# Differential-attention step on one core: queries are projected first, engines write the stacked keys and half of each stacked query tile, and key, query and bias tiles exist twice

## The chip, the core and the metric

The kernel runs on one core of one Trainium2 chip. The metric is the time of one execution on the device in microseconds (us); for the kernel before it is the median of three runs. The profile is one further view of one execution, taken by the hardware profiler.

The core's engines are named as in the profile: PE (TensorE matmul), PEld (its weight load), DVE (VectorE), ACT (ScalarE), POOL (GpSimd) and SP (SyncE, which here issues all DMAs of the program in one order). L212 is line 212 of the kernel.

## The reference

One layer of a hybrid encoder, for 16 meta tokens, 2048 new frames (the prompt) and 32 frames of a running stream (the sample, with 528 cached rows). All arrays are float32.

```python
def diff_attend(q, k, v, q_pos, k_pos, lam, rel_bias):
    s = jnp.einsum('bqhcd,bkhcd->bchqk', q, k, preferred_element_type=f32) * SCALE
    bias = rel_bias[rel_bucket(k_pos[None, :] - q_pos[:, None])]
    s = s + jnp.transpose(bias, (2, 0, 1)).astype(f32)[None, None]
    vis = chunk_id(k_pos)[None, :] <= chunk_id(q_pos)[:, None]
    s = jnp.where(vis, s, NEG)
    p = jax.nn.softmax(s, axis=-1)
    a = p[:, 0] - lam * p[:, 1]
    return jnp.einsum('bhqk,bkhd->bqhd', a.astype(v.dtype), v)

# one layer
q, k, v, z_a, b_g, c_g, u, z_c = split_proj(rmsnorm(hp, norm_g[l]), w_in[l])   # 1024 -> 8 x 512
o = diff_attend(q, k, v, ...)                 # 4 heads, 2 components of 64 per head, values of 128
u_pad = jnp.concatenate([zeros, c_g * u], axis=1)
o = rmsnorm(o, subln_g[l]) * (1 - lam_init) * silu(z_a)
y_c = silu(z_c) * b_g * short_conv(u_pad, conv_w[l])
hp = hp + jnp.concatenate([o, y_c], axis=-1) @ w_out[l]
y_prompt = rmsnorm(hp, final_g)
```

Keys, values and the last convolution rows are outputs too.

## The kernel before

**Precision.** A float32 product is made of three products of a shorter format (float32r): each operand is split into a high part (a cast, written by ACT) and a low part (operand minus high part, by DVE or POOL), and high·high, high·low and low·high are summed in PSUM.

**Stages.** The prompt is worked in four passes `p` of 512 frames (`QT`); pass 0 also holds the 16 meta tokens and the 32 sample frames (560 columns, in two blocks). In a pass, `unit_a(h, p)` projects keys, values, queries and the gate Z of head `h` (in this order), `attend(h, p, st)` does the attention of that head over all frames so far, and `unit_c(u, p)` does the convolution branch of 128 channels with four more projections. A projection (`proj`) of one 128-column weight tile is 24 matmuls per block (8 pieces of the 1024 inputs times three products). After the passes, `out_first` and `out_rest` do the output projection.

**Keys and queries.** A score needs q·k over 64 dimensions of one component `c`. To use all 128 rows of the array, one tile `ks{c}` holds the 64 rows of the keys' high part and, below them, the 64 rows of their low part; `q{c}0` holds the queries' high part twice and `q{c}1` their low part twice. Two matmuls (L428, L429) then give the scores of up to 512 keys. The projections write 128 rows with both components (tiles of the pool `rp`, named `r` in the profile: `kh`, `kl`, `qh`, `ql`), and DMAs move the halves to where they belong:

```python
for c in range(2):
    for i, src in enumerate((kh, kl)):
        if p > 0:
            dma(ks[c][64 * i:64 * i + 64, :k0], ksd[h][i, 64 * c:64 * c + 64, :k0])      # L243
        dma(ks[c][64 * i:64 * i + 64, k0:k0 + kn], src[64 * c:64 * c + 64, :kn])         # L244
...
for half in range(2):
    dma(q2[64 * half:64 * half + 64], src[64 * c:64 * c + 64, f0:f0 + QT])               # L325
```

So a head issues four DMAs `ks<-r`, from pass 1 on four DMAs `ks<-ksd` (keys of the passes before, kept in DRAM as `ksd`), up to pass 2 two DMAs `ksd<-r`, eight DMAs `q<-r`, and one `bz<-bz` (the negated bias of the last 512 columns, L731). `ks0`, `ks1`, the four `q` tiles and `bz` exist once: a DMA that writes them waits until the scores of the head before have read them.

**Scores.** For each tile of 128 queries, `softmax_diff` makes the scores piece by piece into one of three PSUM banks `s`; DVE adds the bias and takes the minimum (L375, last piece) or the minimum alone (L378), ACT writes the exponential (L379), POOL (L382) and DVE (L383) combine both components. A bank is free when ACT has read it.

**Weights.** `w_load` brings a weight tile (`wr`, tag `wraw`, two buffers, 512 KB) and splits it: `wh` by ACT (L191), `wl` by POOL or DVE (L192).

**Order.** A scheduler orders the instructions of each engine at build time by a simulated timeline; code order sets the dependences and the rotation of buffers. Each engine runs its own order strictly, and so does SP's queue: a DMA that waits holds back all DMAs behind it. DMAs use eight semaphores in rotation (`DMAHW0` to `DMAHW7`), so a DMA may also wait for the one eight places ahead.

## Time and profile before

| what | value |
|---|---|
| three runs | 1340.38, 1341.1 and 1345.33 us, median 1341.1 us |
| profiled execution | span 1338.5 us (first to last instruction); its own time is not listed apart from that |
| PE busy | 1285.5 us (96%), 7058 matmul records |
| DVE, ACT, POOL busy | 999.3 (75%), 717.6 (54%), 682.8 us (51%) |
| granted TensorE clock, mean | 0.990 |
| DMA | 215.59 MB, 54.7% of 16 engines' time |

The median of the runs is 2.6 us above the span. In the profile a group row reads: line, engine, operation, output<-inputs, shape, count | busy us, mean ns of one | idle time of the engine before them. A row of waits reads: who waited <- whom for: us in total, times, longest. In a timeline, a bracket at the end of a row is the idle time before it and what ended it.

### The profile page before, as it was taken

To read this page: it belongs to the slowest core of one execution; us is meant where nothing else is said; L and a number is where in the kernel's file an instruction comes from. 1 tells how busy PE (TensorE), PEld (TensorE's weight loads), DVE (VectorE), ACT (ScalarE), POOL (GpSimd) and SP (SyncE) were. 2 spreads that over 40 slices of the span, in tenths; PEclk is the share of its full clock that TensorE was granted. 3 is DMA by queue.
4 is the path that set the end of the run, shared out by engine and by line. 5 is a ranking of instruction groups with operands and counts; after the bars stand their busy time and mean duration, and the time that the engine had idled before them with its cause. 6 is when DMAs were issued, how large, how long until landed. Compare 5 with 4: busy or idle time off the path is not lost.

```text
span 1338.5 us, 21190 instructions
## 1 busy us (share of the span) xinstructions
PE 1285.5 (96%) x7058; PEld 1104.2 (82%) x7058; DVE 999.3 (75%) x2086; ACT 717.6 (54%) x1814; POOL 682.8 (51%) x619
## 2 busy tenths in 40 slices
PE   8899999999999999999999999998999999999997
PEld 6899999977878878878878788887887877878875
DVE  8677676668887958788888898786785895777753
ACT  5554454555564547454645566465554665674432
POOL 4555556455555663565566535564574573452200
PEclk9999999999999999999999999999999999999999
DMA  8754543894445377545453463636247348445851
GB/s 276 229 155 125 164 117 104 245 274 138 139 147 158 103 209 232 141 151 150 150 135 126 120 208 93 167 124 143 94 110 203 117 160 215 165 150 185 273 196 52
DMA packets 118670, 215.59 MB, mean 161 GB/s; under 512 B 19840, under 2 KB 48032, under 8 KB 118560
## 3 DMA queue, kind: packets, MB, share of 16 engines
q1 hardware_dynamic: 118560, 214.23, 54.7%
q8 instruction: 56, 0.92, 0.3%
q14 instruction: 54, 0.44, 0.1%
HBM read 145.62 MB, written 43.26 MB: 141 GB/s over the span
## 4 chain that ended last, share of the span: by engine, by line
PE 59%; DVE 16%; DMA 10%; issue 4%; ACT 4%; POOL 3%; SPq 2%; DVEq 0%; POOLq 0%; ACTq 0%
PE pj L212 37%; PE po L676 6%; DVE p L383 3%; PE s L428 3%; DMA q<-r 3%; PE s L429 3%; PE pt L444 3%; SPq L73 2%; DVE nm L378 2%; PE po L452 2%; PE po L453 2%; PE po L451 2%; DMA ks<-ksd 1%; ACT p L379 1%; POOL wl L192 1%
## 5 line engine op out<-in xcount | busy, mean ns | idle before, releaser
L212 PE MATMUL pj<-xh,wh 128*128 128x512 f32 (+2 forms) x1280 | 457.0, 358 | 4.0 <-ACT wh L191 1.3
L192 POOL TENSOR_TENSOR wl<-wr,wh 128x512 fp32r<-128x512 f32 x240 | 328.7, 1375 | 250.2 <-ACT wh L191 234.7
L212 PE MATMUL pj<-xl,wh 128*128 128x512 f32 (+2 forms) x1280 | 455.1, 356 | 0.8 <-DVE xl L140 0.8
L212 PE MATMUL pj<-xh,wl 128*128 128x512 f32 (+2 forms) x1280 | 454.7, 356 | 0.0
L379 ACT ACTIVATE p<-s,nm 128x384 f32<-128x384 f32 (+5 forms) x352 | 208.8, 595 | 186.8 <-DVE nm L378 135.1
L212 PEld LDWEIGHTS pj<-xh,wh 128*128 128x128 f32 x1280 | 243.2, 190 | 34.2 <-ACT bvec L586 2.0
L212 PEld LDWEIGHTS pj<-xh,wl 128*128 128x128 f32 x1280 | 242.9, 190 | 31.2 <-issue 1.3
L212 PEld LDWEIGHTS pj<-xl,wh 128*128 128x128 f32 x1280 | 243.4, 190 | 30.1 <-DVE xl L140 1.4
L191 ACT CAST wh<-wr 128x512 fp32r<-128x512 f32 x256 | 157.0, 616 | 129.4 <-PE pj L212 78.6
L383 DVE SCALAR_TENSOR_TENSOR p<-p,cf,p 128x384 f32<-128x384 f32 (+5 forms) x176 | 174.5, 1019 | 28.1 <-POOL p L382 27.8
L428 PE MATMUL s<-ks,q 128*128 128x384 f32 (+5 forms) x352 | 129.5, 375 | 26.8 <-DMA q<-r 10.0
L382 POOL TENSOR_SCALAR p<-p,cf 128x384 f32<-128x384 f32 (+5 forms) x176 | 125.0, 726 | 49.2 <-DVE cf L359 35.1
L378 DVE TENSOR_REDUCE nm<-s 128x1 f32<-128x400 f32 (+3 forms) x224 | 122.5, 557 | 28.2 <-PE s L429 27.9
L429 PE MATMUL s<-ks,q 128*128 128x384 f32 (+5 forms) x352 | 124.0, 354 | 2.0 <-DMA q<-r 2.0
L448 DVE TENSOR_TENSOR al<-pt,ah 128x512 fp32r<-128x512 f32 x144 | 97.0, 682 | 37.0 <-ACT ah L447 36.9
L656 POOL TENSOR_TENSOR cll<-ct,chh 128x512 fp32r<-128x512 f32 x40 | 53.9, 1353 | 113.6 <-ACT chh L654 105.4
L428 PEld LDWEIGHTS s<-ks,q 128*128 128x128 f32 x352 | 66.2, 190 | 42.5 <-issue 14.4
L447 ACT CAST ah<-pt 128x512 fp32r<-128x512 f32 x144 | 79.1, 585 | 40.8 <-PE pt L444 40.7
L375 DVE CUSTOM_DVE_ANT_0 s<-s,bz 128x512 f32<-128x512 f32 (+5 forms) x128 | 74.4, 585 | 17.9 <-PE s L429 13.5
L444 PE MATMUL pt<-ident,p 128*128 128x128 f32 x544 | 86.5, 274 | 0.0
L452 PE MATMUL po<-al,vh 128*128 128x256 f32 x288 | 84.2, 292 | 1.9 <-DVE al L448 1.7
L451 PE MATMUL po<-ah,vh 128*128 128x256 f32 x288 | 81.6, 283 | 0.0
(243 smaller groups left out, 2138.4 us busy)
## 6 DMA issues: line engine op xcount, KB each, us to landing
wr<-in_w_in SPq DMA_DIRECT2D x128, 512.0 KB, 4.1
q<-r SPq DMA_DIRECT2D x128, 128.0 KB, 4.7
ct<-cat SPq DMA_DIRECT2D x28, 512.0 KB, 4.8
out<-y SPq DMA_DIRECT2D x32, 256.0 KB, 3.4
ks<-ksd SPq DMA_DIRECT2D x16, 388.0 KB, 7.8
xr<-in_x SPq DMA_DIRECT2D x24, 256.0 KB, 4.8
out<-g SPq DMA_DIRECT2D x24, 256.0 KB, 4.5
xt<-in_xT SPq DMA_DIRECT2D x24, 256.0 KB, 4.2
```

The costliest lines, as they stand in the source:

```text
L191: S.copy(wh, wi)
L192: (V if (col in (CK, CV) if p == 0 else col in (CQ, CZ)) else G).tensor_tensor(wl, wi, f32(wh), op=ALU.subtract)
L212: T.matmul(ps, lhsT=a[:, k % 4], rhs=b[k][:, b0:b1], start=(k == 0 and i == 0), stop=(k == KT - 1 and i == 2))
L378: V.tensor_reduce(nm[:, c, j:j + 1], s, op=ALU.min, axis=AX.X)
L379: S.activation(pr[j][c], s, AF.Exp, bias=nm[:, c, j:j + 1], scale=-1.0, accum_out=l[:, c, j:j + 1])
L382: G.tensor_scalar(a0, a0, cf[:, 0, j:j + 1], 1.0, op0=ALU.mult, op1=ALU.mult)
L383: V.scalar_tensor_tensor(a0, a1, cf[:, 1, j:j + 1], a0, op0=ALU.mult, op1=ALU.add)
L428: T.matmul(ps, lhsT=qd[c][0][:, qs], rhs=ks[c][:, col:col + w], start=True, stop=False)
L429: T.matmul(ps, lhsT=qd[c][1][:, qs], rhs=ks[c][:, col:col + w], start=False, stop=True)
L444: T.transpose(pt[:, i, P * qi:P * (qi + 1)], cols(aa[qi], NM + P * (2 * j + i), P), ident)
L451: T.matmul(po, lhsT=vh[:, kt], rhs=ah[:, i], start=(kt == 0), stop=False)
L452: T.matmul(po, lhsT=vh[:, kt], rhs=al[:, i], start=False, stop=False)
```

## The change

`unit_a` now projects queries first, then keys, values and Z. After a projection, ACT writes the high part of each component directly to its place, in two casts of 64 rows, and POOL the low part in two subtractions of 64 rows. For the keys both parts reach their rows this way: component 0 has its high part in rows 0 to 63 and the low part in rows 64 to 127, component 1 the other way round, so that ACT stays in its rows and POOL writes the other half. For the queries the engines write half of each of the four tiles, and four DMAs of 64 rows copy it to the other half. `ks0`, `ks1`, the `q` tiles and `bz` have two buffers, `wraw` three; the pool `rp` is gone. The past keys come in two DMAs of 128 rows, issued ahead of the key projection; `bz` is loaded ahead of `unit_a`. In pass 0 the low part of the query weights is made by DVE and that of the value weights by POOL (before: value weights by DVE, query weights by POOL). The squares at the start use the key buffers, `post` uses the buffers of `ah` and `al`, and the weights of the second output half use the key and query buffers.

```diff
-    rp = pool("rp", 5)
+    ks_tile = lambda c: kv.tile([P, NK], F32R, tag=f"ks{c}", name=f"ks{c}", bufs=2)
...
-        wr = wp.tile([P, KT, P], F32, tag="wraw", name="wr")
+        wr = wp.tile([P, KT, P], F32, tag="wraw", name="wr", bufs=3)
...
-            (V if (col in (CK, CV) if p == 0 else col in (CQ, CZ)) else G).tensor_tensor(wl, wi, f32(wh), op=ALU.subtract)
+            (V if (col in (CQ, CK) if p == 0 else col in (CQ, CZ)) else G).tensor_tensor(wl, wi, f32(wh), op=ALU.subtract)
...
+        q32 = g_tile(tw)
+        qd = [[one.tile([P, QT], F32R, tag=f"q{c}{i}", name=f"q{c}{i}", bufs=2) for i in range(2)] for c in range(2)]
+        def ev_q(ps, b0, b1):
+            V.scalar_tensor_tensor(q32[:, b0:b1], ps, -0.125, rbs[p][:, b0:b1], op0=ALU.mult, op1=ALU.mult)
+            e = min(b1, f0 + QT)
+            for c in range(2):
+                r = slice(64 * c, 64 * c + 64)
+                hi, lo = (t_[r, b0 - f0:e - f0] for t_ in qd[c])
+                S.copy(hi, q32[r, b0:e])
+                G.tensor_tensor(lo, q32[r, b0:e], f32(hi), op=ALU.subtract)
...
+        proj(CQ + h, p, ev_q)
+        for c in range(2):
+            r, o = slice(64 * c, 64 * c + 64), slice(64 - 64 * c, 128 - 64 * c)
+            for t_ in qd[c]:
+                dma(t_[o], t_[r])
+        k32 = g_tile(tw)
+        ks = [ks_tile(c) for c in range(2)]
+        if p > 0:
+            for c in range(2):
+                dma(ks[c][:, :k0], ksd[h][c, :, :k0])
         def ev_k(ps, b0, b1):
             V.tensor_tensor(k32[:, b0:b1], ps, rbs[p][:, b0:b1], op=ALU.mult)
-            S.copy(kh[:, b0:b1], k32[:, b0:b1])
-            G.tensor_tensor(kl[:, b0:b1], k32[:, b0:b1], f32(kh[:, b0:b1]), op=ALU.subtract)
+            e = min(b1, kn)
+            for c in range(2):
+                r, o = slice(64 * c, 64 * c + 64), slice(64 - 64 * c, 128 - 64 * c)
+                d = slice(k0 + b0, k0 + e)
+                S.copy(ks[c][r, d], k32[r, b0:e])
+                G.tensor_tensor(ks[c][o, d], k32[r, b0:e], f32(ks[c][r, d]), op=ALU.subtract)
         proj(CK + h, p, ev_k)
-        for c in range(2):
-            for i, src in enumerate((kh, kl)):
-                if p > 0:
-                    dma(ks[c][64 * i:64 * i + 64, :k0], ksd[h][i, 64 * c:64 * c + 64, :k0])
-                dma(ks[c][64 * i:64 * i + 64, k0:k0 + kn], src[64 * c:64 * c + 64, :kn])
         if p < NQ - 1:
-            for i, src in enumerate((kh, kl)):
-                dma(ksd[h][i, :, k0:k0 + kn], src[:, :kn])
+            for c in range(2):
+                dma(ksd[h][c, :, k0:k0 + kn], ks[c][:, k0:k0 + kn])
...
-    for col in (CK, CV)[:1]:
-        pre[col, 0] = w_load(col, 0)
+    pre[CQ, 0] = w_load(CQ, 0)
...
+            bz = one.tile([P, 512], F32, tag="bz", name="bz", bufs=2)
+            if (h, p) != (0, 0):
+                dma(bz, bzd[h])
             st = unit_a(h, p)
...
-            st["bz"] = one.tile([P, 512], F32, tag="bz", name="bz", bufs=1)
-            dma(st["bz"], bzd[h])
```

The program issues 630 DMAs instead of 782: 64 instead of 128 copies into `q` tiles, and 24 instead of 112 DMAs into `ks` tiles. How the order moves is shown at three places. In the rows, a number behind a name tells buffers apart.

SP's queue in pass 3 at head 1, before: the query tile `q00_11094` and the key tiles `ks0_10992`, `ks1_10993` wait for PE, that is, for the scores of head 0.

```order
L73 DMA q00_11094<-r_11053 64x512 [waits DMAHW0_49,PE_49]
L73 DMA ks0_10992<-ksd1_132 64x1552 [waits PE_49]
L73 DMA ks0_10992<-r_10951 64x512
L73 DMA ks0_10992<-ksd1_132 64x1552 [waits DMAHW3_49]
L73 DMA ks0_10992<-r_10952 64x512
L73 DMA q00_11094<-r_11053 64x512 [waits DMAHW5_49]
L73 DMA q01_11097<-r_11054 64x512 [waits DMAHW6_49]
L73 DMA q01_11097<-r_11054 64x512 [waits DMAHW7_49]
L73 DMA wr_12025<-in_w_in 128x1024 [waits DMAHW0_49,Pool_49]
L73 DMA ks1_10993<-ksd1_132 64x1552 [waits DMAHW1_49,PE_49]
```

The same head in SP's queue now (`ks0_10889`, `ks1_10890`, `bz_10837` and the tiles `q00_10840` to `q11_10843`).

```order
L72 DMA ks0_10889<-ksd1_129 128x1552 [waits DMAHW5_49,PE_49]
L72 DMA out_4<-g_10671 128x2 [waits DMAHW6_49,DVE_49]
L72 DMA wr_10935<-in_w_in 128x1024 [waits DMAHW7_49,DMAHW2_49,Pool_49]
L72 DMA ks1_10890<-ksd1_129 128x1552 [waits PE_49]
L72 DMA bz_10837<-bz1_301 128x512 [waits DMAHW1_49,DVE_49]
L72 DMA wr_10987<-in_w_in 128x1024 [waits DMAHW3_49,Pool_49]
L72 DMA wr_11581<-in_w_in 128x1024 [waits DMAHW4_49,Pool_49]
L72 DMA cat3_139<-g_10753 512x1x128 [waits DVE_49]
L72 DMA q00_10840<-q00_10840 64x512 [waits DMAHW5_49,Activation_49]
L72 DMA q10_10842<-q10_10842 64x512 [waits DMAHW6_49,Activation_49]
L72 DMA wr_11618<-in_w_in 128x1024 [waits DMAHW7_49,Pool_49]
L72 DMA q01_10841<-q01_10841 64x512 [waits DMAHW0_49,Pool_49]
```

The block of DMAs that followed the last reader of the only buffer is gone: past keys and bias stand well ahead of the query copies, and the query copies wait for the engines that write the first half, no longer for PE.

POOL's order at the same head, before: L236 makes the keys' low part, L314 the queries', L277 the values'.

```order
L192 TENSOR_TENSOR wl_11063<-wr_11056,wh_11062 128x512 [waits PE_49,Activation_49]
L236 TENSOR_TENSOR r_10952<-g_10950,r_10951 128x512 [waits DMAHW3_49,Activation_49]
L192 TENSOR_TENSOR wl_11111<-wr_11108,wh_11110 128x512 [waits DMAHW1_49,PE_49,Activation_49]
L192 TENSOR_TENSOR wl_11115<-wr_11108,wh_11114 128x512 [waits PE_49,Activation_49]
L277 TENSOR_TENSOR vl_10123<-v32_10131,vh_10122 128x512 [waits DMAHW6_49,DVE_49,PE_49]
```

And now (L252 the queries, L278 the keys, L313 the values).

```order
L197 TENSOR_TENSOR wl_10942<-wr_10935,wh_10941 128x512 [waits PE_49,Activation_49]
L252 TENSOR_TENSOR q01_10841<-g_10839,q00_10840 64x512 [waits DMAHW1_49,Activation_49]
L252 TENSOR_TENSOR q11_10843<-g_10839,q10_10842 64x512 [waits Activation_49,Pool_49]
L197 TENSOR_TENSOR wl_10990<-wr_10987,wh_10989 128x512 [waits PE_49,DMAHW2_49,Activation_49,Pool_49]
L197 TENSOR_TENSOR wl_10994<-wr_10987,wh_10993 128x512 [waits PE_49,Activation_49]
L278 TENSOR_TENSOR ks0_10889<-g_10888,ks0_10889 64x512 [waits Activation_49,Pool_49]
L278 TENSOR_TENSOR ks1_10890<-g_10888,ks1_10890 64x512 [waits Activation_49]
L313 TENSOR_TENSOR vl_10065<-v32_10073,vh_10064 128x512 [waits DVE_49,DMAHW5_49,PE_49,Pool_49]
```

Two subtractions stand where one stood, and those of the keys stand behind two weight subtractions (L197) that wait for ACT and PE.

SP's queue at the start, before: `wr_421` is the weight tile of the values, the second that PE needs.

```order
L73 DMA bd0_294<-bvec_171 128x383 [waits DMAHW7_49,Activation_49]
L73 DMA bd1_302<-bvec_175 128x383 [waits DMAHW0_49,Activation_49]
L73 DMA kts_415<-in_ckT 128x512 [waits DMAHW1_49]
L73 DMA bd2_310<-bvec_179 128x383 [waits DMAHW2_49,Activation_49]
L73 DMA ktn_417<-in_ckT 128x16 [waits DMAHW3_49]
L73 DMA wr_421<-in_w_in 128x1024 [waits DMAHW4_49]
```

And now: `wr_416` belongs to the keys, `wr_496` to the values, which PE still takes second.

```order
L72 DMA bd0_287<-bvec_168 128x383 [waits DMAHW7_49,Activation_49]
L72 DMA bd1_295<-bvec_172 128x383 [waits DMAHW0_49,Activation_49]
L72 DMA wr_416<-in_w_in 128x1024 [waits DMAHW1_49]
L72 DMA bd2_303<-bvec_176 128x383 [waits DMAHW2_49,Activation_49]
L72 DMA kts_490<-in_ckT 128x512 [waits DMAHW3_49]
L72 DMA ktn_492<-in_ckT 128x16 [waits DMAHW4_49]
L72 DMA wr_496<-in_w_in 128x1024 [waits DMAHW5_49]
```

The value weights have one more weight tile in front of them.

More of the change, by code (lines that the diff above doesn't have):

```diff
@@ L124, in x_rms, with sqt @@
         rbs[p] = rb
-    sqt = lambda n: rp.tile([P, 560], F32, tag="r", name="sq")[:, :n]
+    def sqt(k, n):
+        if k == 0:
+            sqs[:] = [f32(t_)[:, 560 * j:560 * (j + 1)] for t_ in [ks_tile(c) for _ in range(2) for c in range(2)] for j in range(3)]
+        return sqs[k][:, :n]
+    sqs = []
     def x_load(p):
@@ L236, in ev_k @@
-            G.tensor_tensor(kl[:, b0:b1], k32[:, b0:b1], f32(kh[:, b0:b1]), op=ALU.subtract)
+            e = min(b1, kn)
[4 more added lines that the diff above has]
+                G.tensor_tensor(ks[c][o, d], k32[r, b0:e], f32(ks[c][r, d]), op=ALU.subtract)
         proj(CK + h, p, ev_k)
         dma(kT_p[h, :, k0:k0 + kn], k32[:, :kn])
-        ks = [kv.tile([P, NK], F32R, tag=f"ks{c}", name=f"ks{c}") for c in range(2)]
@@ L240, in unit_a @@
[L240 to L244 removed]
         if p < NQ - 1:
[L246 to L247 removed]
+            for c in range(2):
+                dma(ksd[h][c, :, k0:k0 + kn], ks[c][:, k0:k0 + kn])
@@ L303, in unit_a @@
         st["v"] = (vh, vl)
-        qh, ql, q32 = r_tile(tw), r_tile(tw), g_tile(tw)
-        qs = None
-        if p == 0:
-            qs = one.tile([P, 2 * NS], F32, tag="qs", name="qs")
-            G.memset(qs, 0.0)
-        def ev_q(ps, b0, b1):
-            V.scalar_tensor_tensor(q32[:, b0:b1], ps, -0.125, rbs[p][:, b0:b1], op0=ALU.mult, op1=ALU.mult)
-            S.copy(qh[:, b0:b1], q32[:, b0:b1])
-            G.tensor_tensor(ql[:, b0:b1], q32[:, b0:b1], f32(qh[:, b0:b1]), op=ALU.subtract)
-            if p == 0 and b1 == tw:
-                for c in range(2):
-                    V.tensor_copy(qs[64 * c:64 * c + 64, NS * c:NS * (c + 1)], q32[64 * c:64 * c + 64, smp])
-        proj(CQ + h, p, ev_q)
-        qd = []
-        for c in range(2):
-            pair = []
-            for i, src in enumerate((qh, ql)):
-                q2 = one.tile([P, QT], F32R, tag=f"q{c}{i}", name=f"q{c}{i}")
-                for half in range(2):
-                    dma(q2[64 * half:64 * half + 64], src[64 * c:64 * c + 64, f0:f0 + QT])
-                pair.append(q2)
-            qd.append(pair)
-        st["q"] = qd
-        st["qs"] = qs
         z32, l1 = g_tile(tw), g_tile(tw)
@@ L631, in w_half @@
         else:
-            ks = [kv.tile([P, NK], F32R, tag=f"ks{c}", name=f"wo{c}") for c in range(2)]
+            ks = [ks_tile(c) for c in range(2)]
             his = [ks[k // 4][:, 512 * (k % 4):512 * (k % 4 + 1)] for k in range(KT)]
-            los = [r_tile(512) for _ in range(4)]
-            los += [one.tile([P, QT], F32R, tag=f"q{c}{i}", name=f"wq{c}{i}") for c in range(2) for i in range(2)]
+            los = [one.tile([P, QT], F32R, tag=f"q{c}{i}", name=f"wq{c}{i}", bufs=2) for _ in range(2) for c in range(2)
+                   for i in range(2)]
         for k in range(KT):
@@ L643, in load_cat @@
     def load_cat(t, rows, spare=False):
-        ct = wp.tile([P, KT, P], F32, tag="wraw", name="ct")
+        ct = wp.tile([P, KT, P], F32, tag="wraw", name="ct", bufs=3)
         dma(ct[:, :, :rows], cat_s if t == 16 else cat[t // 4][:, t % 4])
```

21 lines of the change are left out of this document (15 added, 6 removed).

## The prediction, made before the changed kernel was run

> **What bounds the kernel now.** I read the page's head first: busy times of the engines, the granted clock in 40 slices, and the chain of work that ended last, by engine.
>
> ```profile
> PE 1285.5 (96%) x7058; PEld 1104.2 (82%) x7058; DVE 999.3 (75%) x2086; ACT 717.6 (54%) x1814; POOL 682.8 (51%) x619
> PEclk9999999999999999999999999999999999999999
> PE 59%; DVE 16%; DMA 10%; issue 4%; ACT 4%; POOL 3%; SPq 2%; DVEq 0%; POOLq 0%; ACTq 0%
> ```
>
> PE is the bound, and the change takes no matmul away. So a gain can come from PE's idle 53.0 us (1338.5 - 1285.5) and from what idling does to the matmuls behind it, and from nothing else. Second view: PE's waits, longest in total first (total us, times, longest).
>
> ```profile
> PE s L428 <- DMA q<-r: 10.0, 6, 3.2
> PE s L428 <- ACT p L379: 8.6, 11, 2.1
> PE s L428 <- DMA bz<-bz: 4.9, 1, 4.9
> PE pv L584 <- DMA oh<-in_ohd: 4.0, 1, 4.0
> PE s L428 <- DMA ks<-r: 2.5, 1, 2.5
> PE s L429 <- DMA q<-r: 2.0, 5, 0.6
> ```
>
> Scores (`s`) that wait for DMAs of `q`, `ks` and `bz` are 10.0 + 4.9 + 2.5 + 2.0 = 19.4 us in 13 waits, the largest group; `oh` is the start of the program and stays. Third view: the timeline of SP's queue and of PE at one of these places, head 1 of pass 3.
>
> ```profile
> 1012.74 0.50 SPq L73 DMA_DIRECT2D q<-r  x1
> 1013.29 0.59 SPq L73 DMA_DIRECT2D ks<-ksd  x1
> ...
> 1020.24 0.59 SPq L73 DMA_DIRECT2D ks<-ksd  x1
> 1022.15 0.46 SPq L73 DMA_DIRECT2D ks<-r  x1
> 1022.75 1.15 SPq L73 DMA_DIRECT2D q<-r  x2
> ...
> 1020.22 0.39 PE L212 MATMUL pj<-xl,wh 128*128 128x512 f32 x1
> 1023.34 0.42 PE L428 MATMUL s<-ks,q 128*128 128x400 f32 x1 [2.73 <-DMA q<-r]
> ...
> 1026.32 0.63 PE L212 MATMUL pj<-xh,wl 128*128 128x512 f32 x1
> ...
> 1028.11 0.40 PE L212 MATMUL pj<-xh,wl 128*128 128x512 f32 x1
> ```
>
> The reader is to see two things. The DMAs into the single buffers begin only when the head before is done with them and take more than 10 us in SP's one queue; PE has filler work for 7.9 us of that and then stands. And after the stall a matmul of 512 columns lasts 0.63 instead of 0.40 us: the clock. Fourth view: the granted clock in the stretches behind three of these stalls, and in a quiet one (us, busy time of the engines, PEclk, DMA share, GB/s).
>
> ```profile
> 501.00:505.00 4.00, 3.91 (x11) 3.12 (x12) 2.00 (x4) 2.43 (x5) 0.00 (x0) 0.57 1.03 304
> 1023.80:1027.20 3.40, 3.40 (x10) 2.62 (x9) 0.00 (x0) 0.59 (x1) 0.00 (x0) 0.50 1.01 210
> 1122.90:1126.00 3.10, 3.10 (x9) 2.40 (x8) 3.10 (x5) 1.21 (x3) 1.45 (x1) 0.50 1.03 217
> 508.00:512.00 4.00, 4.00 (x20) 3.35 (x19) 2.72 (x7) 2.87 (x10) 0.00 (x0) 1.00 0.62 200
> ```
>
> **The change, part by part.**
>
> *A. Waits for q, ks and bz: -21.6 us.* With two buffers, past keys and bias are asked for a head earlier, and new keys need no DMA at all. The query copies no longer wait for PE, and are four instead of eight. What is late next at these places is the engine chain behind a projection (C). The idle time is 19.4 us. A wait also hides the tail of the matmul ahead of it, since matmuls overlap:
>
> ```profile
> L212 PE MATMUL pj<-xh,wh 128*128 128x512 f32 x768 | 305.6, 399 | 0.0
> 1130.72 4.16 PE po L676 x18
> ```
>
> One lasts 0.399 us, but 18 in a row take 4.16, 0.231 each; 13 waits hide 13 x (0.399 - 0.231) = 2.2 us more. Bounds: 0 (all waits are replaced) and 21.6. I take all of it here and count the replacement in C.
>
> *B. Half clock behind the stalls: -5.0 us.* In the three stretches the lost time is stretch x (1 - clock): 4.00 x 0.43 + 3.40 x 0.50 + 3.10 x 0.50 = 5.0 us. Bounds 0 (another stall at the same places) and 5.0; I take 5.0, because the clock is 1.00 wherever PE runs on. [...]
>
> *C. Double casts and subtractions: +5.1 us.* The number of splits doubles; the rows of before are these.
>
> ```profile
> L235 ACT CAST r<-g 128x512 fp32r<-128x512 f32 (+1 forms) x20 | 10.9, 543 | 8.7 <-DVE g L234 8.7
> L313 ACT CAST r<-g 128x512 fp32r<-128x512 f32 (+1 forms) x20 | 10.7, 536 | 3.5 <-DVE g L312 2.9 <-DMA ks<-ksd 0.6
> L236 POOL TENSOR_TENSOR r<-g,r 128x512 fp32r<-128x512 f32 (+1 forms) x20 | 23.8, 1190 | 64.9 <-ACT r L235 43.1 <-DMA ks<-r 16.5 <-DMA xr<-in_x 5.3
> L314 POOL TENSOR_TENSOR r<-g,r 128x512 fp32r<-128x512 f32 (+1 forms) x20 | 23.4, 1168 | 4.6 <-ACT r L313 3.9 <-POOL wl L192 0.7
> q<-r SPq DMA_DIRECT2D x128, 128.0 KB, 4.7
> ```
>
> No row shows these with 64 rows; I take the time to go with the columns, as the full price (half of it is the other bound, if it went with the rows). ACT then gets 20 x 0.543 + 20 x 0.536 = 21.6 us more (739, 55% of the span), POOL 20 x 1.190 + 20 x 1.168 = 47.2 us more (730, 55%). Neither binds by its sum. On the path they show only as a longer chain: for keys DVE's evacuation (taken as long as a cast, 0.54) + two casts 1.1 + two subtractions 2.4 = 4.0 us, for queries 4.7 more for the DMA, 8.7 us. The cover is the projections that stand between: queries have keys and values behind them (48 matmuls of 0.231, 11 us), keys have the values' 24 (5.5 us), and longer where scores of the head before are mixed in. In the order, the thinnest cover is the first head of pass 1 with the values' 24 matmuls, a few of the keys' and some ten small products between its queries and its first score, some 8 us; there the copies may come 1 us late. New keys are also needed last, in the last piece of a row of scores. If the cover were gone, each of the 16 heads would pay up to 4 us.
> What stays is that ACT and DVE, which until now caught up while PE stood, are now the next to be late. The price of such a wait is the row of ACT above, 8.6 / 11 = 0.78 us. I let half of the 13 places have one: 13 x 0.5 x 0.78 = 5.1 us. Bounds: 0, and the longest such wait at all 13, 13 x 2.1 = 27.3.
>
> *D. Start: +1 us.* PE's second projection, the values, now has one more weight tile ahead of its own in SP's queue and in ACT's, and its low part comes from POOL.
>
> ```profile
> 20.83 1.14 ACT L191 CAST wh<-wr 128x512 fp32r<-128x512 f32 x2 [3.62 <-DMA wr<-in_w_in]
> 25.15 2.53 POOL L192 TENSOR_TENSOR wl<-wr,wh 128x512 fp32r<-128x512 f32 x2 [8.64 <-ACT wh L191]
> 22.68 2.05 PE L158 MATMUL pss<-sq,ones 128*128 128x280 f32 x8
> ```
>
> The casts begin when the weights land, 20.83; with 1.14 us of casts for the keys' tile ahead, POOL's first subtraction would end near 20.83 + 1.14 + 0.57 + 1.27 = 23.8, the second near 25.1. PE comes to the values at 24.4, behind the squares' sums, and reaches the second half of the weights some 1.5 us later. So 0 to 2 us are lost, and I take 1.
>
> *E. At nothing.* The third `wraw` buffer: a PE wait for `wh` is not among the longest, shown above, and ACT's waits for weights lie beside PE's matmuls. The fewer bytes in the DMA queue: hidden as long as PE does not wait for a DMA. `post` in the buffers of `ah`: its matmuls and copies lie between two heads, where PE has projections. The second half of the output weights, which can load earlier: in PE's rows above there is no wait for it.
>
> The sum is -21.6 - 5.0 + 5.1 + 1.0 = -20.5 us on a span of 1338.5. The median of the runs is 1341.1, 2.6 us above the span; on it the sum gives 1320.6, which I round to 1321.
>
> **Rivals.**
>
> *R1, the wait changes its name (no change).* [...] These copies of DVE differ in little but their place in time:
>
> ```profile
> L317 DVE COPY qs<-g 64x32 f32<-64x32 f32 x8 | 6.6, 821 | 0.2
> L515 DVE COPY g<-hist 128x2 f32<-128x2 f32 x16 | 3.6, 226 | 0.0
> ```
>
> A copy of 32 columns that takes 0.821 us stood beside something, and L317 follows in the code right on POOL's subtraction of the queries' low part (L314). The price: 13 places with a wait midway between 0.78 and 2.1, 1.44 us, 18.7 us in all, and the clock halved behind them as now: -21.6 + 18.7 = -2.9, 1338 us. Against it: even if DVE stood through all 47.2 us, it would be busy 1046.5 us, 78% of the span. [...]
>
> *R2, POOL's queue holds back the keys (slower).*
>
> ```profile
> POOL wl L192 <- ACT wh L191: 234.7, 112, 8.6
> L192 POOL TENSOR_TENSOR wl<-wr,wh 128x512 fp32r<-128x512 f32 x240 | 328.7, 1375 | 250.2 <-ACT wh L191 234.7 <-ACT nm L354 6.3 <-PE pj L212 4.4
> ```
>
> For: in POOL's strict order the keys' two subtractions stand behind two weight subtractions, which wait for ACT 234.7 / 112 = 2.1 us a time. Two of them uncovered in front of the keys, 2 x 1.375 = 2.75 us at all 16 heads, is 44 us: -26.6 + 44 = +17.4, 1358 us. It decides from 26.6 / 16 = 1.7 us per head. Against: the pair already stood ahead of the keys before, and POOL is idle 45% of the time.
>
> *R3, nothing comes back (faster still).* C at 0 and D at 0, and half of ACT's 8.6 us go too, because scores start at an even pace: -26.6 - 4.3 = -30.9, 1310 us. For: 11 waits on ACT come partly behind the stalls. Against: ACT has more to do.
>
> **How the numbers follow.** My forecast (1313 to 1331) has 0.62, R1 0.16, R2 0.08, R3 0.14. The range of 8 in 10 reaches from 1306, a little below R3, to 1338, R1; outside lie R2 and the ends of R1 and R3. 0.5% of 1341.1 is 6.7 us, about what a measurement tells from no change: faster is below 1334.4. Forecast, R3 and the better end of R1 give 0.79 faster; the rest of R1 and the start of R2 0.14 the same; R2 0.07 slower.
>
> **What would show it.** A: no PE wait for `q`, `ks` or `bz` above 1 us, PE busy about 97.5% of the span. B: PEclk 1.00 around the heads' first scores. C: 40 casts and 40 subtractions each for queries and keys, about 0.54 and 1.18 us each; PE's waits for ACT and DVE together grow by about 5 us. D: PE's idle time in the first 40 us within 2 us of now. Wrong: PE waits for POOL's `ks` rows (R2), or idle time of PE as large as before under new names (R1).

## The result, and the profile after

The changed kernel takes 1328.78 us (median of 4 runs, 1327.2 to 1330.27); beside it on the same chip the kernel before took 1343.21 us (1340.38 to 1346.31). The ratio is 0.9889, with a 95% interval of 0.9864 to 0.9914: faster by 1.1%. The profiled execution has a span of 1327.7 us, 10.8 less than before. The kernel before has 57 more runs, beside the experiments below: their spans lie 1.7 to 1.9 us under their times, and their median is 1344.9 us. The profile before, with a span of 1338.5, thus belongs to a run of some 1340.3 us, and the two profiles show only 10.8 of the 14.4 us between the medians.

First the head of the page: busy times, granted clock, and the chain of work that ended last.

```profile
PE 1281.4 (97%) x7058; PEld 1105.9 (83%) x7058; DVE 1000.8 (75%) x2086; ACT 740.3 (56%) x1854; POOL 732.1 (55%) x659
...
PEclk9999999999999999899999999999999999999999
...
PE 69%; DVE 17%; ACT 5%; DMA 4%; issue 3%; POOL 1%; SPq 1%; DVEq 0%; ACTq 0%; POOLq 0%
```

PE is still the bound. DMA fell from 10% to 4% of the chain; DVE stayed, and is now what PE meets next. The same shows in PE's waits (us in total, times, longest).

```profile
PE po L686 <- DVE y L687: 5.4, 4, 2.1
PE s L438 <- ACT p L389: 5.3, 8, 3.3
PE pv L594 <- DMA oh<-in_ohd: 4.6, 1, 4.6
PE pt L454 <- DVE p L393: 4.3, 4, 2.5
PE ptv L308 <- DVE g L297: 3.9, 4, 2.2
...
PE s L439 <- DMA q<-q: 2.0, 1, 2.0
```

Of the 13 waits of scores for DMAs one is left, `q<-q`. Adding up all rows of this view by who is waited for:

| PE waits for | before, us (times) | after, us (times) |
|---|---|---|
| DMA at the start (`oh`) | 4.0 (1) | 4.6 (1) |
| other DMAs | 19.4 (13) | 2.0 (1) |
| ACT | 11.5 (14) | 5.9 (9) |
| DVE | 8.6 (16) | 25.6 (24) |
| POOL and issue | 0.6 (2) | 0 |

The 10.8 us of the span add up so: -17.4 (other DMAs), -5.6 (ACT), +17.0 (DVE), +0.6 (start), -0.6 (POOL and issue), -0.7 (gaps too short for this view; PE's idle time as a whole went from 53.0 to 46.3), and -4.1 (PE's busy time).

### The profile page after: what moved, and what is told of

It reads as the page before. It is cut to its first block, busy times and chain, and to the rows that moved or that the text cites. A ratio compares the mean times of both kernels' runs of the same rounds, so it can differ in the third digit from the quotient of the medians.

```text
span 1327.7 us, 21145 instructions
## 1 busy us (share of the span) xinstructions
PE 1281.4 (97%) x7058; PEld 1105.9 (83%) x7058; DVE 1000.8 (75%) x2086; ACT 740.3 (56%) x1854; POOL 732.1 (55%) x659
## 4 chain that ended last, share of the span: by engine, by line
PE 69%; DVE 17%; ACT 5%; DMA 4%; issue 3%; POOL 1%; SPq 1%; DVEq 0%; ACTq 0%; POOLq 0%
PE pj L217 40%; PE po L686 9%; PE pt L454 3%; PE s L438 3%; PE s L439 3%; DVE p L393 3%; PE po L462 2%; PE po L463 2%; PE po L461 2%; DMA out<-y 2%; DVE nm L388 2%; ACT p L389 1%; DMA xt<-in_xT 1%; DVE al L458 1%; ACT wh L196 1%
## 5 line engine op out<-in xcount | busy, mean ns | idle before, releaser
L197 POOL TENSOR_TENSOR wl<-wr,wh 128x512 fp32r<-128x512 f32 x240 | 329.7, 1378 | 258.1 <-ACT wh L196 248.2
L217 PEld LDWEIGHTS pj<-xh,wl 128*128 128x128 f32 x1280 | 244.1, 191 | 30.9 <-issue 1.1
L217 PEld LDWEIGHTS pj<-xl,wh 128*128 128x128 f32 x1280 | 244.4, 191 | 30.3 <-DVE xl L145 1.4
L393 DVE SCALAR_TENSOR_TENSOR p<-p,cf,p 128x384 f32<-128x384 f32 (+5 forms) x176 | 168.5, 984 | 16.1 <-POOL p L392 15.1
L388 DVE TENSOR_REDUCE nm<-s 128x1 f32<-128x384 f32 (+3 forms) x224 | 122.6, 559 | 14.9 <-PE s L439 14.6
L385 DVE CUSTOM_DVE_ANT_0 s<-s,bz 128x512 f32<-128x512 f32 (+5 forms) x128 | 73.8, 588 | 12.8 <-PE s L439 10.2
L463 PE MATMUL po<-ah,vl 128*128 128x256 f32 x288 | 81.1, 282 | 0.0
```

Of the source, the lines that this page charges most:

```text
L197: (V if (col in (CQ, CK) if p == 0 else col in (CQ, CZ)) else G).tensor_tensor(wl, wi, f32(wh), op=ALU.subtract)
L217: T.matmul(ps, lhsT=a[:, k % 4], rhs=b[k][:, b0:b1], start=(k == 0 and i == 0), stop=(k == KT - 1 and i == 2))
L388: V.tensor_reduce(nm[:, c, j:j + 1], s, op=ALU.min, axis=AX.X)
L393: V.scalar_tensor_tensor(a0, a1, cf[:, 1, j:j + 1], a0, op0=ALU.mult, op1=ALU.add)
```

## One stall in the trace: DVE behind POOL

The longest new wait, 3.28 us, stands under ACT's name. Timeline of POOL, DVE and PE around it (start us, us, engine, line, operation; in brackets the idle time before):

```profile
527.20 2.94 POOL L278 TENSOR_TENSOR ks<-g,ks 64x512 fp32r<-64x512 f32 x2 [0.18 <-ACT ks L277]
530.23 1.27 POOL L197 TENSOR_TENSOR wl<-wr,wh 128x512 fp32r<-128x512 f32 x1
```

```profile
528.93 1.24 DVE L174 TENSOR_TENSOR x<-x,x 128x4 f32<-128x4 f32 x1
530.09 0.15 DVE L367 RECIPROCAL r<-M 128x2 f32<-128x2 f32 x1
...
530.28 1.23 DVE L368 TENSOR_TENSOR r<-r,lam 128x2 f32<-128x2 f32 x1
531.43 0.69 DVE L385 CUSTOM_DVE_ANT_0 s<-s,bz 128x512 f32<-128x512 f32 x1
```

```profile
529.48 0.29 PE L439 MATMUL s<-ks,q 128*128 128x272 f32 x1
533.04 0.60 PE L438 MATMUL s<-ks,q 128*128 128x272 f32 x1 [3.28 <-ACT p L389]
...
535.54 0.63 PE L217 MATMUL pj<-xl,wh 128*128 128x512 f32 x1
```

Two multiplications of 4 and 2 columns take 1.24 and 1.23 us on DVE. The first ends when POOL's pair of key subtractions ends (530.17 against 530.14), the second when POOL's weight subtraction ends (531.51 against 531.50). The minimum over a score bank (L385) is queued behind them, ACT's exponential behind that, and PE has no bank until 533.04. Then matmuls last 0.63 instead of 0.40 us: half clock (the granted clock from 535 to 538 us is 0.50). The groups of the second multiplication (two inputs) and of the reciprocal (one), both of 2 columns, show that size does not decide which is lengthened:

```profile
L368 DVE TENSOR_TENSOR r<-r,lam 128x2 f32<-128x2 f32 x52 | 20.9, 402 | 1.3
...
L367 DVE RECIPROCAL r<-M 128x2 f32<-128x2 f32 (+1 forms) x56 | 9.1, 163 | 1.5
```

The same multiplication by lambda is run 56 times: the 31 with no POOL instruction beside them average 159 ns, the 24 with POOL beside them for over half of their time 736 ns, up to 1270. The reciprocal stays at 162 to 164 ns in both cases. The number of inputs alone does not decide it either: of the 16 copies L542, with one input and again 2 columns, the five with no POOL instruction beside them take 154 to 171 ns, the eight with POOL there for over half of their time 169 to 1044. Of L363, L365 and L368, 65 instructions last over 0.4 us, and each ends 9 to 29 ns after a POOL instruction does.

Summed over all of DVE (each instruction beyond the tenth percentile of its own form, where that is over 0.1 us) this is 207 us of its busy time before and 210 after. Each of these instructions has a POOL instruction beside it for at least 80% of its excess. So the wait was there before the change and the change did not add to it: even behind POOL's subtractions of keys and queries, whose time doubled, DVE lost 16.7 us before and 16.0 after. What changed is where PE meets it. Of PE's 24 waits for DVE, 18 have a DVE instruction lengthened in this way within them or in the 2 us before them; the four for `y` at the output, 5.4 us, have none.

## The experiments

All medians are of runs on a chip that also ran the kernel before (1344 to 1346 us there); "waits" are PE's, in us, without the start.

| kernel | median us | ratio, 95% interval | DMA / ACT / DVE waits |
|---|---|---|---|
| before, double splits alone | 1370.33 | 1.0185 [1.0155, 1.0216] | 22.7 / 14.2 / 25.6 |
| before, two buffers alone | 1348.19 | 1.0021 [1.0004, 1.0038] | 5.2 / 17.1 / 23.4 |
| before, queries first alone | 1350.31 | 1.0037 [1.0020, 1.0054] | 7.2 / 13.5 / 30.3 |
| before, neutral edit | 1342.76 | 0.9978 [0.9962, 0.9994] | 16.6 / 12.4 / 12.0 |
| changed, neutral edit | 1329.90 | 0.9885 [0.9866, 0.9905] | 2.1 / 5.9 / 26.9 |
| changed, one buffer in use | 1329.06 | 0.9880 [0.9855, 0.9905] | 0 / 4.8 / 27.4 |
| changed, past keys late in the code, one key buffer | 1327.85 | 0.9884 [0.9855, 0.9914] | 0.2 / 5.5 / 30.9 |
| changed, queries by DMA | 1336.05 | 0.9943 [0.9921, 0.9966] | 5.5 / 7.3 / 27.2 |
| changed, low parts on DVE | 1342.17 | 0.9975 [0.9959, 0.9991] | 3.1 / 10.1 / 31.2 |
| changed, DVE lightened | 1345.08 | 1.0007 [0.9988, 1.0026] | 2.0 / 14.6 / 25.4 |
| changed, keys first | 1355.75 | 1.0076 [1.0050, 1.0102] | 5.0 / 12.7 / 32.2 |
| changed, keys by DMA | 1358.06 | 1.0098 [1.0076, 1.0120] | 10.2 / 13.4 / 28.2 |

A caution holds for all of them. The scheduler plans anew for each kernel. I compared the sequence of DVE's instructions (source line and tiles) with that of the parent kernel, block by block with the longest match first. PE, DVE, ACT and POOL have identical sequences for the two neutral edits and for "one buffer in use"; 75% of DVE's instructions fall into matching blocks for "past keys late", 65% for "queries by DMA", 56% for "low parts on DVE" and "DVE lightened", 49% for "keys by DMA", 32% for "keys first", and 59, 52 and 43% for the first three rows against the kernel before. (The longest sequence in common, with gaps allowed, is 69 to 85% of the instructions in these.) Only the first group changes one thing alone.

**Double splits alone.** The kernel before with two casts and two subtractions of 64 rows where one of 128 rows stood, for keys and queries.

```diff
-            S.copy(kh[:, b0:b1], k32[:, b0:b1])
-            G.tensor_tensor(kl[:, b0:b1], k32[:, b0:b1], f32(kh[:, b0:b1]), op=ALU.subtract)
+            for r in (slice(0, 64), slice(64, 128)):
+                S.copy(kh[r, b0:b1], k32[r, b0:b1])
+                G.tensor_tensor(kl[r, b0:b1], k32[r, b0:b1], f32(kh[r, b0:b1]), op=ALU.subtract)
```

> The kernel before, with nothing changed but the splits: keys and queries are cast in two casts of 64 rows and their low part is made in two subtractions of 64 rows, 40 more of each on ACT and POOL (some 47 us more on POOL). DMAs, buffers and order of the code stay. Theory 1 (POOL's extra subtractions hold up DVE, and PE then waits for DVE): PE's waits for DVE grow by 8 us or more, 1348 to 1355 us. Theory 2 (DVE is late only because PE no longer pauses for DMAs): the DMA waits still cover it, within 3 us of before, 1340 to 1346 us. A subtraction of 64 rows takes as long as one of 128, about 1.2 to 1.3 us for 512 columns.

It costs 25 us, more than either theory expected and five times the term C of the prediction. PE's waits for DVE are 25.6 us, three times those of before, the DMA waits stay, and PE's busy time is 10 us longer (1295.6 us; 13 windows of half clock, described below, against seven). ACT (741.4 us) and POOL (731.1 us) are as busy as in the changed kernel, so the same work costs much less there; that it is paid there out of the stalls that went is a reading, and not shown. How much of the 25 us is the work and how much the new order, this run does not tell.

**Low parts on DVE.** The changed kernel with both kinds of 64-row subtractions on DVE instead of POOL.

```diff
-                G.tensor_tensor(lo, q32[r, b0:e], f32(hi), op=ALU.subtract)
+                V.tensor_tensor(lo, q32[r, b0:e], f32(hi), op=ALU.subtract)
...
-                G.tensor_tensor(ks[c][o, d], k32[r, b0:e], f32(ks[c][r, d]), op=ALU.subtract)
+                V.tensor_tensor(ks[c][o, d], k32[r, b0:e], f32(ks[c][r, d]), op=ALU.subtract)
```

> The changed kernel, with the low parts of keys and queries made by DVE instead of POOL. DVE gets 80 instructions of some 0.4 to 0.7 us more (about 45 us), POOL loses about 95 us. Theory 1 (POOL's subtractions hold up DVE): PE's waits for DVE fall from 25 to about 12 us, 1314 to 1322 us. Theory 2 (DVE itself is the next to be late): they grow, 1330 to 1340 us.

```profile
PE 1283.7 (96%) x7058; PEld 1103.7 (82%) x7058; DVE 1052.7 (79%) x2166; ACT 740.5 (55%) x1854; POOL 644.1 (48%) x579
```

POOL lost 88 us, DVE gained 52, and the kernel is 13 us slower than the changed one; PE waits for DVE 31.2 instead of 25.6 us. That fits theory 2, DVE's queue as the next late one, and is a little more than it expected; the order differs too, so the price of the move by itself is not shown.

**DVE lightened.** The opposite: three operations of one input go from DVE to ACT.

```diff
-        V.tensor_copy(vh[:, new], v32)
+        S.copy(vh[:, new], v32)
...
-        V.tensor_copy(sqh, sq)
+        S.copy(sqh, sq)
...
-        V.tensor_scalar(yc, ch[:, :bn - 2], cw[:, 0, u:u + 1], None, op0=ALU.mult)
+        S.activation(yc, ch[:, :bn - 2], AF.Copy, scale=cw[:, 0, u:u + 1])
```

> The changed kernel with three operations of one input moved from DVE to ACT: the cast of the new values' high part, the cast of the squares' high part in post, and the first product of the convolution. DVE loses 16 x 0.57 + 20 x 0.61 + 16 x 0.62 = 31 us of its 1001, ACT gains about 30 us of its 740. Theory 'DVE is late next' (what PE now waits for is DVE by its load; 52 us more on DVE cost 13 us in an earlier run): 31 us less give back some 8 us, about 1321 us, and PE's waits for DVE fall from 25.6 to about 18 us. Theory 'ACT is as late as DVE': the waits change their name to ACT, and the time stays within 3 us of 1328.8. Theory 'noise of the schedule': anything within 6 us to both sides, with no relation to the engines' loads.

```profile
PE 1285.0 (96%) x7058; PEld 1102.4 (82%) x7058; DVE 1003.1 (75%) x2034; ACT 767.7 (57%) x1906; POOL 734.2 (55%) x659
```

```profile
PE s L438 <- ACT p L389: 11.5, 12, 3.6
```

This is a miss for the theory that DVE's load decides: 31 us of work left DVE, its busy time rose by 2.3 us, and the kernel is 16 us slower. Much of what left came back as waiting behind POOL: the sum of the section above is 226 us here, against 210, although the three operations took some 9 us of it away with them. ACT, with 27 us more, came late for PE: 14.6 instead of 5.9 us. The order differs as well, so how the 16 us divide is open. But neither DVE's nor ACT's share of busy time (75% and 56%) foretold what a few operations more or less cost.

**One buffer in use.** The changed kernel, in which every head takes the same one of the two buffers of `ks`, `q` and `bz`.

```diff
-        ks = [ks_tile(c) for c in range(2)]
+        ks = [(ks_tile(c), ks_tile(c))[1] for c in range(2)]
```

(and likewise for the `q` tiles and `bz`)

> The changed kernel, but each head uses the same one of the two buffers of the key tiles, the query tiles and the bias, so that they have a single buffer again; direct writes, four query copies and the order stay. If the second buffer is what took PE's DMA waits away: they come back with 10 to 20 us, 1338 to 1350 us. If the direct writes and the fewer DMAs did it: DMA waits stay under 5 us, 1327 to 1333 us.

1329.06 against 1328.78 us, with the same order on every engine: the second buffers bring nothing. PE's stalls stand at the same places (2.55 us at 341 and 342, 2.24 and 2.25 at 809 and 811, 1.90 at 1099 and 1100), and no wait for a DMA is left but the start's; where the changed kernel waits 1.99 us for `q<-q`, this one waits 1.49 for POOL.

**Two buffers alone.** The kernel before with two buffers for `ks` and `q` (and, to make room, `post` in the buffers of `ah` and `al`, four `r` tiles instead of five, five `xt` tiles instead of six, and the smaller scratch).

```diff
-        ks = [kv.tile([P, NK], F32R, tag=f"ks{c}", name=f"ks{c}") for c in range(2)]
+        ks = [kv.tile([P, NK], F32R, tag=f"ks{c}", name=f"ks{c}", bufs=2) for c in range(2)]
...
-                q2 = one.tile([P, QT], F32R, tag=f"q{c}{i}", name=f"q{c}{i}")
+                q2 = one.tile([P, QT], F32R, tag=f"q{c}{i}", name=f"q{c}{i}", bufs=2)
```

> The kernel before, with two buffers for the key and the query tiles and nothing else of the change in the data path (bias single; to make room, the pool of the projections has four buffers instead of five, the pool of inputs five instead of six, and the square parts use the buffers of ah and al). If the second buffer is what counts: PE's DMA waits fall from 19 us to under 6, 1325 to 1332 us. If the eight query copies behind a late query projection are what counts: they stay above 10 us, 1336 to 1344 us.

Here the DMA waits do fall, from 19.4 to 5.2 us, and no time is gained, which neither theory expected: DVE's waits rise from 8.6 to 23.4 us, and ACT's from 11.5 to 17.1. It may be that a wait that ended last hid others, which now end last; the smaller pools and the new order could have brought them too, and no run tells these apart.

**Two neutral edits.** The query copies in another order, in the changed kernel and in the kernel before.

```diff
-        for c in range(2):
+        for c in (1, 0):
             r, o = slice(64 * c, 64 * c + 64), slice(64 - 64 * c, 128 - 64 * c)
             for t_ in qd[c]:
                 dma(t_[o], t_[r])
```

```diff
-                for half in range(2):
+                for half in (1, 0):
                     dma(q2[64 * half:64 * half + 64], src[64 * c:64 * c + 64, f0:f0 + QT])
```

> The changed kernel with the four query copies issued for component 1 first, then 0. No work, buffer or dependence changes; only the order that the scheduler finds may. Theory 'noise of the schedule' (a part of every difference measured here is the luck of the order): it moves by 3 us or more from the changed kernel's 1328.8 us, and PE's waits stand at other places. Theory 'structure': within 2 us of 1328.8, and PE's idle time by releaser stays at about DMA 2.6, ACT 5.9 and DVE 25.6 us.

> The kernel before with the eight query copies of a head issued lower half first in each pair, then upper half. Nothing else changes. Theory 'noise of the schedule': the kernel before is one draw of many, and this one differs from 1341 to 1345 us by 5 us or more; it tells how much of the measured 14 us the change owns. Theory 'structure': within 2 us, with PE waits for DMA of 20 to 27 us and for DVE of about 9 us as before.

Both stay within 2.3 us of their parents. They were meant to shuffle the order and did not (PE, DVE, ACT and POOL keep theirs), so they show how well a given order repeats, and not how far two orders differ.

**Which part of the change.** Three kernels do or undo one part: the kernel before with queries first (their tiles, projection and copies now ahead of the keys'); the changed kernel with keys as before (128-row parts, DMAs `ks<-r` and `ks<-ksd`, one key buffer); the changed kernel with queries as before (128-row parts, eight copies, one buffer).

```diff
-    for col in (CK, CV)[:1]:
-        pre[col, 0] = w_load(col, 0)
+    pre[CQ, 0] = w_load(CQ, 0)
...
+        proj(CQ + h, p, ev_q)
         k32, kh, kl = g_tile(tw), r_tile(tw), r_tile(tw)
```

> The kernel before with one part of the change: queries are projected first (with the weights of the start and DVE's share of the weight subtractions as in the changed kernel). Keys and queries still go through 128-row tiles and DMAs, all in one buffer; one cast and one subtraction each, so ACT and POOL have no extra work. Theory 'order carries the gain' (undoing the order in the changed kernel cost 26 us): about 1325 to 1330 us, and PE's waits for DMAs into q are gone or nearly; those for ks stay or grow, since keys now have the values' and Z's projections behind them. Theory 'order helps only where the engines write the tiles': the query copies still wait in SP's queue for the only buffer, and the time stays at 1337 to 1345 us with PE waits for DMA of 15 us or more.

```diff
-                S.copy(ks[c][r, d], k32[r, b0:e])
-                G.tensor_tensor(ks[c][o, d], k32[r, b0:e], f32(ks[c][r, d]), op=ALU.subtract)
+            S.copy(kh[:, b0:b1], k32[:, b0:b1])
+            G.tensor_tensor(kl[:, b0:b1], k32[:, b0:b1], f32(kh[:, b0:b1]), op=ALU.subtract)
...
+                if p > 0:
+                    dma(ks[c][64 * i:64 * i + 64, :k0], ksd[h][i, 64 * c:64 * c + 64, :k0])
+                dma(ks[c][64 * i:64 * i + 64, k0:k0 + kn], src[64 * c:64 * c + 64, :kn])
```

> The changed kernel with the keys as before: one cast and one subtraction of 128 rows into tiles r, then four DMAs ks<-r and from pass 1 on four ks<-ksd, with ks0 and ks1 in one buffer. Queries stay first and half written by engines. POOL gets some 23 us less, ACT 11 us less than in the changed kernel. Theory 'direct key writes carry the gain': PE waits for DMAs into ks come back, 10 us or more, and the time is 1337 us or above. Theory 'order carries the gain, the extra work on POOL and ACT costs': POOL's 23 us less bring back a part of the 27 us that the doubled work cost in the kernel before, and the time is 1316 to 1326 us.

```diff
-                S.copy(hi, q32[r, b0:e])
-                G.tensor_tensor(lo, q32[r, b0:e], f32(hi), op=ALU.subtract)
+            S.copy(qh[:, b0:b1], q32[:, b0:b1])
+            G.tensor_tensor(ql[:, b0:b1], q32[:, b0:b1], f32(qh[:, b0:b1]), op=ALU.subtract)
...
+                for half in range(2):
+                    dma(q2[64 * half:64 * half + 64], src[64 * c:64 * c + 64, f0:f0 + QT])
```

> The changed kernel with the queries as before: one cast and one subtraction of 128 rows into tiles r, and eight copies into the q tiles, which have one buffer; the low weights of the second output half use r tiles and one g tile. Queries stay first, keys stay direct. POOL gets some 24 us less, ACT 11 us less than in the changed kernel. Theory 'order gives the copies cover enough': no more PE waits for DMA than in the changed kernel plus 3 us, and with less on POOL 1318 to 1327 us. Theory 'four copies instead of eight matter': PE waits for q 8 us or more, 1335 us or above.

Queries first alone makes the kernel before 6 us slower, which neither theory expected: the waits for `q` are gone, and those for the past keys come instead. In sum PE's waits for DMA fall to 7.2 us, and those for DVE rise to 30.3.

```profile
PE s L428 <- DMA ks<-ksd: 5.8, 4, 2.3
```

With keys by DMA the changed kernel loses all its gain and 14 us more. SP's queue and PE at head 1 of pass 3 there:

```profile
1019.88 0.49 SPq L73 DMA_DIRECT2D ks<-ksd  x1
1020.42 0.59 SPq L73 DMA_DIRECT2D ks<-r  x1
...
1025.54 0.46 SPq L73 DMA_DIRECT2D ks<-r  x1
1026.95 0.33 SPq L73 DMA_DIRECT2D bz<-bz  x1
1027.59 4.64 SPq L73 DMA_DIRECT2D q<-q  x4
...
1034.71 0.67 PE L439 MATMUL s<-ks,q 128*128 128x400 f32 x1 [3.81 <-DMA ks<-ksd]
```

Eight DMAs into the key tiles are issued one behind the other, and PE stands at the end of them. The PE waits of that kernel for keys are these.

```profile
PE s L439 <- DMA ks<-ksd: 8.1, 4, 3.8
...
PE s L439 <- DMA ks<-r: 2.1, 1, 2.1
```

Both signs of the theory "direct key writes carry the gain" are there, but these waits are not the whole loss: the span is 25.4 us longer than that of the changed kernel, and the waits for DMA are 8.2 us of this. Waits for ACT are 7.5 more, for DVE 2.6, for POOL and issue 3.2, and PE's busy time is 4.7 us longer.

Queries by DMA cost only 7 us, with `q<-r` waits of 5.5 us, less than the 8 that one theory asked for and more than the other allowed. POOL has 27 and ACT 12 us less to do, and the kernel is still slower. So half of POOL's extra work given back did not pay for eight copies and the order that came with them; what it is worth by itself this run does not show.

**Keys first.** The changed kernel with the order keys, values, queries, Z: the queries' tiles, projection and copies stand behind the values', and the weights of the start match that.

```diff
-    pre[CQ, 0] = w_load(CQ, 0)
+    pre[CK, 0] = w_load(CK, 0)
...
+        proj(CQ + h, p, ev_q)
         z32, l1 = g_tile(tw), g_tile(tw)
```

> The changed kernel with one part undone: the projections of a head stand again in the order keys, values, queries, Z, and the first weights are those of the keys. Direct writes, four query copies and two buffers stay. Theory 'order' (the waits for query copies went because queries are projected 48 matmuls earlier, and so have 11 us of cover more): the copies are late again in passes 1 to 3, PE waits for DMA by 8 us or more, and the time is about 1337 us. Theory 'fewer and direct DMAs' (the waits went because keys need no DMA behind the projection, and a query copy is no longer behind others in SP's queue): Z's 24 matmuls, 5.5 us, cover the four copies nearly, PE waits for DMA stay below 4 us in total outside the start, and the time is 1327 to 1333 us.

27 us slower than the changed kernel, beyond both theories: DMA waits of 5.0 us are 3 more, ACT's and DVE's are 6.8 and 6.6 more, and PE's busy time is 9 us longer (ten windows of half clock, below, against seven). Direct writes in the old order lose 11 us against the kernel before, queries first with the old writes 6; together they gain 14. The order of the engines' work, the least alike of all these kernels (32% of DVE's instructions in matching blocks), can't be told apart from the transfers in this run.

**Past keys late in the code.** To split the loss of "keys by DMA": the changed kernel with one key buffer in use and the DMAs of past keys behind the key projection in the code.

```diff
-        ks = [ks_tile(c) for c in range(2)]
-        if p > 0:
-            for c in range(2):
-                dma(ks[c][:, :k0], ksd[h][c, :, :k0])
+        ks = [(ks_tile(c), ks_tile(c))[1] for c in range(2)]
...
         proj(CK + h, p, ev_k)
+        if p > 0:
+            for c in range(2):
+                dma(ks[c][:, :k0], ksd[h][c, :, :k0])
```

> The changed kernel with the keys' tiles as in the kernel of single buffers (1329.1 us) and, as the one edit beyond that, the two DMAs of past keys behind the key projection in the code instead of ahead of it. The kernel whose keys came by DMA took 1358.1 us: it had 128-row parts with four DMAs for the new keys, past keys in four DMAs behind the projection, and one buffer. Theory 'direct writes of the new keys' (the 29 us come from the DMAs behind the projection and their place in SP's queue): moving the past keys back costs little, 1327 to 1335 us, PE waits for ks<-ksd below 3 us. Theory 'early past keys' (the gain is that 0.3 to 1.5 MB per head are asked for earlier): 1342 us or more, with PE waits for ks<-ksd of 6 us or more, as the 8.1 us of that kernel.

```profile
PE s L439 <- DMA q<-q: 0.2, 1, 0.2
```

1327.85 us, and no wait for keys at all. That shows again that the second buffer doesn't carry the gain. It does not show the same of the early load, because the transfers did not become late. By SP's rows the first DMA of past keys is issued 27 to 97 us ahead of DVE's evacuation of the new keys, in each of the 12 heads of passes 1 to 3; in the changed kernel it is 24 to 105 us ahead. In "keys by DMA" it goes from 46 us ahead to 91 behind, in the kernel before from 29 ahead to 102 behind. So what stands against the 1358 us of "keys by DMA" is the direct write (with 24 instead of 112 DMAs into the key tiles), the early past keys and another order, all three together.

## Why the prediction was right, and where not

The forecast of 1321 us with a range of 1306 to 1338 held 1328.78; it was 7.8 us too low. That it held is owed to the width of the range: B and C were both too favourable, by 5.0 and 6.3 us. By its steps:

- **A, waits for `q`, `ks`, `bz`: right in size, in part wrong in its reason.** The idle time of 19.4 us fell to 2.0. The text put a part of this on two buffers; "one buffer in use" shows that one is enough, and "two buffers alone" that two are no gain. Its other reasons stand, though not one by one: the engines' direct writes leave two key DMAs per head that scores wait for, and they are issued ahead of the key projection; and queries first gives the copies cover (with keys first, the waits for `q<-q` are 5.1 us instead of 2.0). The two rows that carry it, with KB each and us to landing:

```profile
q<-q SPq DMA_DIRECT2D x64, 128.0 KB, 3.4
ks<-ksd SPq DMA_DIRECT2D x8, 776.0 KB, 6.1
```

- **B, half clock: failed.** It expected 5.0 us back. There were seven stretches of 3.41 us at half clock in the body of the trace before and seven after, at the new stalls. Other runs do not give the 5 us back either: the granted clock is 0.989 in the mean of the 57 runs of the kernel before, and 0.989 in that of the 12 runs of the changed kernel and the two with its order. One of the stretches after (us, busy time of the engines, PEclk, DMA share, GB/s):

```profile
535.00:538.00 3.00, 3.00 (x9) 2.43 (x8) 2.04 (x8) 1.26 (x6) 0.60 (x2) 0.50 0.79 271
```

- **C, doubled casts and subtractions: the engines right, the path mis-sized.** Cost goes with the columns, as taken: 64 rows last as long as 128. With 512 columns a cast takes 0.62 us (before, with 128 rows, 0.62) and a subtraction 1.41 and 1.36 us (before 1.43 and 1.36); the means in these rows mix that with the narrower blocks of pass 0.

```profile
L252 POOL TENSOR_TENSOR q<-g,q 64x512 fp32r<-64x512 f32 (+2 forms) x40 | 47.7, 1193 | 18.4 <-ACT q L251 16.8
L278 POOL TENSOR_TENSOR ks<-g,ks 64x512 fp32r<-64x512 f32 (+2 forms) x40 | 44.9, 1121 | 9.1 <-ACT ks L277 6.6
...
L277 ACT CAST ks<-g 64x512 fp32r<-64x512 f32 (+2 forms) x40 | 21.4, 535 | 11.9 <-DVE g L272 11.3
L251 ACT CAST q<-g 64x512 fp32r<-64x512 f32 (+2 forms) x40 | 21.3, 533 | 8.5 <-DVE g L246 7.9
```

  ACT gained 22.7 us (21.6 forecast), POOL 49.3 (47.2). But C let half of 13 places wait 0.78 us for ACT, +5.1. Measured: ACT's waits fell by 5.6, DVE's rose by 17.0, together +11.4, with a mean of 25.6 / 24 = 1.07 us for DVE. The text named DVE beside ACT as the next to be late, but took the price and the number of places from ACT's row alone, the engine that got the work. With B at 0 and C at 11.4 its own sum would have been -21.6 + 11.4 + 1.0 = -9.2 us; the span fell by 10.8. The place it named as the thinnest cover, the first head of pass 1, is where the one DMA wait is left, 1.99 us at 282 us (1 us forecast).

- **D, the start: +1 us forecast, +0.4 found, by other parts.** Windows of the two kernels, before first, then after:

```profile
0.00:60.00 60.00, 50.45 (x305) 44.54 (x306) 40.74 (x95) 31.83 (x74) 27.98 (x33) 1.00 0.83 255
60.00:250.00 190.00, 189.59 (x1470) 184.10 (x1470) 127.09 (x316) 91.89 (x240) 111.09 (x113) 1.00 0.53 145
```

```profile
0.00:60.00 60.00, 53.94 (x337) 47.90 (x338) 46.01 (x121) 38.92 (x97) 35.11 (x42) 1.00 0.88 279
60.00:250.00 190.00, 185.68 (x1429) 181.07 (x1428) 123.02 (x289) 88.86 (x229) 117.67 (x118) 0.99 0.45 124
```

  PE's idle time in the first 60 us fell from 9.55 to 6.06, and rose from 0.41 to 4.32 in the rest of pass 0. The late value weights that it counted on are no wait of PE.

- **E, at nothing:** right for `wraw` and the bytes. At the output PE's wait for DVE's residual sum (`po` for `y`) rose from 1.9 to 5.4 us; the weights themselves are on time, as said.

- **The rivals.** R1, the wait that changes its name, came near in its sum and not in its places: DVE's waits rose by 17.0 us where R1 had 18.7 at the heads' first scores. None of the 24 waits for DVE is before a score. They stand before projections, transposes and value products, and 4.8 of the 17.0 us before the output projection (7.3 against 2.5 in the kernel before), which never waited for a DMA. That the added work on POOL would hold DVE up more is not borne out, since DVE lost 207 us to POOL before and 210 after. It did not decide, because ACT's waits fell by 5.6 us (R3 had 4.3 of it) and PE's busy time by 4.1. Of these 4.1, A had 2.2 as the tails of 13 waits; eleven waits fewer in all give 11 x 0.168 = 1.8 us by the same reckoning, and the rest I did not trace. R2 did not come: PE has no wait for POOL's `ks`.

What stays open: how much of the 7 to 29 us that the partial kernels lose is the order that the scheduler happened on, and which of direct writes, fewer DMAs and early past keys took PE's waits for DMA away. No run here held the order and changed the work, or the other way round, except the three with an identical order.

## What to carry to other kernels

A group of stalls by one cause is an upper bound: ask which engine is late next, and price it by that engine's own waits. Here 17.4 us of stalls for DMA went, and 11.4 came back as waits for ACT and DVE together. Before buying a second buffer, look whether a transfer can leave the chain between projection and use; here the second buffers brought nothing. And where a scheduler plans the order, compare the orders first: only kernels with the same order on the engines price one part of an edit alone.
